# One decoder layer on one core: an input norm without GpSimd, high parts on ScalarE, and three issue points moved

## The chip, the cores and the metric

The kernel runs on one core of a Trainium2 chip. The metric is the device time of one execution in microseconds (us); the time of a kernel is the median of its runs. All rows come from the hardware profiler's record of one execution. PE is TensorE's matmuls, PEld its weight loads, DVE is VectorE, ACT ScalarE, POOL GpSimd, and SPq the queue of SyncE, which issues the transfers.

## The reference

One layer of a decoder, with 1024 tokens and width 1024. What matters here:

```python
h = rmsnorm(x, norm_mix)                       # x * rsqrt(mean(x*x) + eps) * g
fq, fk, fv, ff, su, hq, hf, hi, hg, gl = split(h @ w_in)
y_fox = fox_attention(rmsnorm(fq), rmsnorm(fk), fv, log_sigmoid(ff + b))  # 8 heads x 64, causal
y_s5  = s5_mixer(su, ...)                      # 32 groups, diagonal complex state space, gelu, glu
y_hg  = hgrn2_mixer(hq, hf, hi, hg, ...)       # 4 heads, gated linear recurrence
gates = sigmoid(gl)                            # three of them, 1024 wide each
merged = gates[0]*(y_fox @ wb0) + gates[1]*(y_s5 @ wb1) + gates[2]*(y_hg @ wb2)
x = x + merged @ w_out
x = x + cross_attention(rmsnorm(x), rmsnorm(mem), ...)
x = x + swiglu(rmsnorm(x), w_gate_up, w_down)
```

## The kernel before

Everything is float32 in effect: an operand is split into a high part (a copy rounded to the format that TensorE takes fast, `fp32r`) and a low part (the operand less its high part), and a product of two is three matmuls, high by high, high by low, low by high (`projs`, line 383). The high part is usually a copy on ScalarE and the low part a subtraction on VectorE (`split`, line 264). Tensors lie with channels on the 128 partitions and the 1024 tokens along the free axis; a matmul works on 512 tokens at most. All tiles come from one arena of 50 slots of 128 x 1024 floats (`u`), and all PSUM tiles from 8 banks (`psm`).

The work is written as generators. A main generator (first the state space, then attention, then the recurrence) yields after each stage, with a weight; `drive` (line 334) then calls `pump`, which takes that weight times a constant, in us of matmul work as the program counts it, from a queue of fillers: projections of the normed input, which need nothing of the main line. In this way TensorE has work while VectorE and ScalarE carry a chain. `later(us, fn)` puts off a piece until so much more matmul work has been issued. `ahead(n, fn)` issues a piece under a place n instructions earlier than where it stands. From these places a planner makes the order of instructions on each engine; each engine then works strictly in that order.

The places that the change touches, in order of time:

- `load_x` (line 475) loads the 8 blocks of x one after the other and splits them with the norm's gain. It also forms the sum of squares: for even blocks ScalarE squares and VectorE adds into `acc`, for odd ones GpSimd multiplies and adds into `accg` (named `sq` in the profile). In `run` (line 1342 on) the first two projections, `su0` and `su1`, run over all 8 blocks; behind them `acc` and `accg` are merged and `row_scale` makes the norm's factor `Rb` with a matmul by ones (tile `rs`). All later matmuls stand behind that one.
- `s5_main` (line 1231): for 8 groups of the state space, `s5_prep` (lag 0, GpSimd), `s5_out` (lag 3), `s5_prep2` (lag 1) and `s5_body` (lag 2) are issued in this order in each round o = 0 to 10, and after each the weight `S5_W[lag]` times 4.5 us of fillers. `s5_body` ends with the carried states `kcs` on VectorE, which `s5_out`'s matmuls (tile `s5y`) read one round later. In rounds 8 to 10 there is no `s5_prep`.
- `fox_main` (line 742): 16 units of attention (4 pairs of heads, 2 halves of the queries, 2 heads), each over 4 or 8 blocks of 128 keys. A step is a matmul for the scores (`st`), an exponential on ScalarE (`pf`), its high part on GpSimd and its low part on VectorE (both in `pt`), an addition into the row sums on GpSimd (`facc`), and, two steps later (`PV_LAG`), the matmul with the values (`pv`). The largest score of each row for the next unit is found beside this by `fox_pre` (line 683): matmuls `mx`, maxima on VectorE, then `chain`, four small operations which fill `mc`, and `rows`, which transposes `mc` with TensorE (tile `mt`). After a unit `fox_out` splits the row sums (`ah`), and `sums` adds them over the partitions with a matmul (`sm`).
- `run`, lines 1403 to 1407: gate 1 (branch of the state space) and then gate 2 (branch of the recurrence). Before gate 2, `load_parts` (line 1681) loads the four heads' outputs (`ldy`) and splits them into `yh` and `yl`. In gate 1 GpSimd adds the product into the merged output `mg` through a strided view.

Of the kernel before, what the change touches and what calls it, by code (L numbers as in the profile page):

```python
# [10 lines left out]
F32 = mybir.dt.float32  # L11
# [8 lines left out]
P = 128  # L20
# [32 lines left out]
S5_US = 4.5  # L53
S5_W = (1.0, 0.6, 1.0, 1.2)
FOX_AT = 8
# [17 lines left out]
FOXL_T = 8.0  # L73
MIX_US = 8.5
EPS = 1e-6
NEG = -1e30
# [117 lines left out]
class Trunk:  # L194
# [280 lines left out]
    def load_x(self):  # L475
# [3 lines left out]
        self.xl = [self.u(f"xl{k}", F32R) for k in range(KB)]  # L479
        acc, accg = self.u("acc"), self.u("sq")  # L480
        _, ap, shape = self.wlist[0]
        raw, hi, lo = self.u("wr", F32, shape), self.u("wh", F32R, shape), self.u("wl", F32R, shape)
        self.wraw[0], self.wrdy[0] = raw, (hi, lo)

        def square(k, xk):
            if k % 2 == 0:
                self.sq_add(xk, acc, k, eng=nc.vector)
                return
            sq = accg if k == 1 else self.u("sq")
            self.mul(sq, xk, xk, nc.gpsimd)  # L490
            if k > 1:
                self.add(accg, accg, sq, nc.gpsimd)

        last = None
        for k in range(KB):
            xk = self.u("xk")
            cuts = [slice(0, NT)] if k else [slice(0, 512), slice(512, NT)]
            if k == 0:
                nc.sync.dma_start(out=raw[:, 0:2], in_=ap[:, 0:2])
            for c in cuts:  # L500
                nc.sync.dma_start(out=xk[:, c], in_=self.io["xT"][k][:, c])
            if k == 0:
                nc.sync.dma_start(out=raw[:, 2:], in_=ap[:, 2:])
                self.w_load(1)
                self.split(raw[:, 0:2], hi[:, 0:2], lo[:, 0:2])
            for c in cuts:
                self.split_gain(xk[:, c], self.par("norm_mix", k), self.xh[k][:, c], self.xl[k][:, c])
            if k == 0:
                self.split(raw[:, 2:], hi[:, 2:], lo[:, 2:])
                del self.wraw[0]  # L510
                self.w_prep(1)
            else:
                square(k - 1, last)
            last = xk
        self.w_load(2)
        square(KB - 1, last)
        return acc, accg

# [164 lines left out]
    def fox_pre(self, un):  # L683
# [6 lines left out]
        def build():  # L690
# [4 lines left out]
            st["pm"] = self.sp.tile([P, 4, 2], F32, tag="pmx", name="pmx")  # L695
            st["mn"] = self.sp.tile([P, 4], F32, tag="mn", name="mn")

        def piece(i, c):
# [17 lines left out]
        def chain():  # L716
            mn = st["mn"]
            if half == 1:
                self.nc.vector.tensor_reduce(out=mn, in_=st["pm"], axis=AX.X, op=ALU.max, negate=True)
            mc = self.sp.tile([P, 4, 16], F32, tag="mc", name="mc")  # L720
            mh = self.sp.tile([P, 4], F32R, tag="mh", name="mh")
            self.nc.gpsimd.tensor_copy(out=mc, in_=self.ohc[:, hd].unsqueeze(1).to_broadcast([P, 4, 16]))
            self.nc.vector.tensor_copy(out=mh, in_=mn)
            self.nc.vector.tensor_copy(out=mc[:, :, 8], in_=mh.bitcast(F32))
            self.sub(mc[:, :, 9], mn, mh.bitcast(F32))
            st["mc"] = mc

# [7 lines left out]
        for i in range(4):  # L735
            for c in range(1 if half == 0 else 2):
                out.append(piece(i, c))
        return out + [chain, rows]

    hi_pool = (0, 1, 2, 3)  # L740

    def fox_main(self):
# [11 lines left out]
        for ui, un in enumerate(units):  # L754
# [17 lines left out]
            for j in range(nj):  # L772
# [11 lines left out]
                pt = self.u("pt", F32R).rearrange("p (a b) -> p a b", a=2)  # L784
                if j % 4 in self.hi_pool:
                    self.ts(pt[:, 0, q0:512], pr, 1.0, 0.0, ALU.mult, ALU.add, self.nc.gpsimd)
                else:
                    self.act(pt[:, 0, q0:512], pr, AF.Copy)
                self.sub(pt[:, 1, q0:512], pr, pt.bitcast(F32)[:, 0, q0:512])
# [28 lines left out]
    def fox_out(self, un, o, acc):  # L818
# [26 lines left out]
        if h == 1:  # L845
            self.later(2.0, sums)
        if half == 1 and h == 1:
# [482 lines left out]
    def run(self, stop=None):  # L1330
# [10 lines left out]
        self.plan_rest()  # L1341
        xs = self.load_x()
        self.setup2()
        g = self.projs([(f"su{i}", self.su_evac(i)) for i in range(2)], self.rx)
        for k, _ in enumerate(g):
            if k == 3:
                acc, accg = xs
                self.stt(acc, accg, 1.0 / 1024.0, acc, ALU.mult, ALU.add)
                self.Rb = self.row_scale(acc)
                self.Rt = self.cp.tile([P, 8], F32, name="Rt")  # L1350
                self.later(8.0, lambda: self.col_scale(self.Rb, self.Rt, 8))
        xs = acc = accg = None
        self.filler("su", self.su_projs())
# [48 lines left out]
        zt = None  # L1402
        self.filler("gate1", self.gates(1, ys))
        self.finish()
        ys = None
        self.filler("gate2", self.gates(2, self.load_parts([self.hy_d[h] for h in range(4)])))
        self.finish()
# [248 lines left out]

    def gates(self, b, y):
        for ob in range(8):
            yield from self.gate(b, ob, y)

    def glu(self, zt, y):
# [18 lines left out]

    def load_parts(self, srcs):
        out = []
        for s in srcs:
            t = self.u("ldy")
            self.nc.sync.dma_start(out=t, in_=s)
            h, l = self.u("yh", F32R), self.u("yl", F32R)
            self.split(t, h, l)
            out.append((h, l))
        return out

# [650 lines left out]
```

## Time and profile before

| what | value |
|---|---|
| median of 3 timed runs | 2130.84 us (2130.14 to 2133.14) |
| the profiled execution | 2138.17 us |
| its span, first to last instruction | 2136.1 us |
| mean granted clock of TensorE | 0.992 |
| TensorE busy | 2079.2 us, 97% |
| VectorE busy | 1521.9 us, 71% |
| ScalarE busy | 814.8 us, 38% |
| GpSimd busy | 608.2 us, 28% |

Busy times are sums over the whole span; what an engine waits for is read from the stretch where it waits. A line of a helper such as `mul` or `act` is shared by many operations, so tiles tell them apart. The granted clock is given as a share of full speed (2.4 GHz; 0.50 is 1.2 GHz).

### The profile page before, as it was taken

To read this page: it belongs to the slowest core of one execution; us is meant where nothing else is said; L and a number is where in the kernel's file an instruction comes from. 1 tells how busy PE (TensorE), PEld (TensorE's weight loads), DVE (VectorE), ACT (ScalarE), POOL (GpSimd) and SP (SyncE) were. 2 spreads that over 40 slices of the span, in tenths; PEclk is the share of its full clock that TensorE was granted. 3 is DMA by queue.
4 is the path that set the end of the run, shared out by engine and by line. 5 is a ranking of instruction groups with operands and counts; after the bars stand their busy time and mean duration, and the time that the engine had idled before them with its cause. 6 is when DMAs were issued, how large, how long until landed. Compare 5 with 4: busy or idle time off the path is not lost.

```text
span 2136.1 us, 26862 instructions
## 1 busy us (share of the span) xinstructions
PE 2079.2 (97%) x10044; PEld 1706.7 (80%) x10044; DVE 1521.9 (71%) x2229; ACT 814.8 (38%) x1268; POOL 608.2 (28%) x551
## 2 busy tenths in 40 slices
PE   7998999999999999999999999999999999999999
PEld 5887777776788878888778888878788888888887
DVE  8887898888854566545675567656897778775772
ACT  4113345545531123215434445444533333344441
POOL 4281204454543223221722100011032324221320
PEclk9999999999999999999999999999999999999999
DMA  4332221110213233235554523334232322248582
GB/s 163 137 104 74 51 75 32 40 50 30 70 46 124 73 109 123 74 99 196 194 192 154 201 92 106 119 117 135 74 120 98 124 99 99 103 150 282 189 281 99
DMA packets 121042, 250.94 MB, mean 117 GB/s; under 512 B 15816, under 2 KB 53704, under 8 KB 120912
## 3 DMA queue, kind: packets, MB, share of 16 engines
q1 hardware_dynamic: 120912, 249.23, 34.2%
q8 instruction: 79, 1.29, 0.3%
q14 instruction: 51, 0.42, 0.1%
HBM read 184.83 MB, written 63.18 MB: 116 GB/s over the span
## 4 chain that ended last, share of the span: by engine, by line
PE 59%; DVE 4%; DMA 1%; ACT 1%; issue 0%; SPq 0%; DVEq 0%; ACTq 0%
PE fp L228 27%; PE pj L228 26%; PE hs L228 2%; PE xo L228 1%; PE xs L228 1%; PE rs L228 1%; PE ho L228 0%; DVE t L246 0%; DVE tl L246 0%; DVE gate L246 0%; DMA gate<-gz_d 0%; DVE yl L246 0%; DMA wr<-xv 0%; DMA ldy<-hy_d 0%; PE xt L233 0%
## 5 line engine op out<-in xcount | busy, mean ns | idle before, releaser
L228 PE MATMUL pj<-xl,wh 128*128 128x512 f32 x784 | 315.5, 406 | 4.7 <-DVE xl L258 4.6
L228 PE MATMUL pj<-xh,wh 128*128 128x512 f32 x784 | 313.3, 405 | 6.7 <-ACT xh L243 5.8
L228 PE MATMUL pj<-xh,wl 128*128 128x512 f32 x784 | 311.7, 401 | 0.0
L246 DVE TENSOR_TENSOR wl<-wr,wh 128x1024 fp32r<-128x1024 f32 (+2 forms) x138 | 170.4, 1236 | 58.5 <-ACT wh L243 56.2
L228 PE MATMUL fp<-th,wc 128*128 128x512 f32 x640 | 206.9, 389 | 0.0
L228 PE MATMUL fp<-hh,wc 128*128 128x512 f32 x644 | 191.4, 389 | 0.0
L228 PEld LDWEIGHTS pj<-xh,wh 128*128 128x128 f32 x784 | 149.2, 190 | 40.0 <-ACT xh L243 6.1
L228 PEld LDWEIGHTS pj<-xl,wh 128*128 128x128 f32 x784 | 148.5, 190 | 37.4 <-DVE xl L258 7.1
L228 PEld LDWEIGHTS pj<-xh,wl 128*128 128x128 f32 x784 | 149.1, 190 | 30.8 <-issue 1.9
L228 PE MATMUL fp<-fx,wc 128*128 128x512 f32 x720 | 172.9, 389 | 0.0
L243 ACT ACTIVATE wh<-wr 128x1024 fp32r<-128x1024 f32 (+2 forms) x138 | 131.8, 957 | 76.8 <-DMA wr<-w_in 50.3
L228 PEld LDWEIGHTS fp<-fx,wc 128*128 128x128 f32 x720 | 135.2, 188 | 28.0
L228 PEld LDWEIGHTS fp<-hh,wc 128*128 128x128 f32 x644 | 120.9, 188 | 25.0
L228 PEld LDWEIGHTS fp<-th,wc 128*128 128x128 f32 x640 | 120.2, 188 | 24.9
L246 DVE TENSOR_TENSOR wc<-wr,wc 128x512 fp32r<-128x512 f32 (+1 forms) x116 | 108.5, 954 | 31.4 <-ACT wc L243 31.4
L246 POOL TENSOR_TENSOR dm<-dm 128x256 f32<-128x256 f32 (+1 forms) x96 | 79.5, 828 | 179.9 <-DMA dm<-w_dn 163.0
L246 POOL TENSOR_TENSOR acc<-acc,sq 128x512 f32<-128x512 f32 (+1 forms) x18 | 30.7, 1706 | 340.5 <-ACT sq L243 340.4
L228 PE MATMUL fp<-tl,wc 128*128 128x512 f32 x320 | 124.6, 389 | 0.7 <-DVE tl L246 0.7
L246 DVE TENSOR_TENSOR pt<-pf,pt 128x512 fp32r<-128x512 f32 (+1 forms) x96 | 94.4, 985 | 40.2 <-POOL pt L262 39.9
L246 POOL TENSOR_TENSOR fc<-fc,fs 128x512 f32<-128x512 f32 x40 | 58.0, 1449 | 216.2 <-ACT fs L243 216.2
L228 PE MATMUL fp<-hl,wc 128*128 128x512 f32 x280 | 108.9, 389 | 0.0
L262 POOL TENSOR_SCALAR pt<-pf 128x512 fp32r<-128x512 f32 (+1 forms) x96 | 67.7, 706 | 139.0 <-ACT pf L243 127.8
(427 smaller groups left out, 4862.3 us busy)
## 6 DMA issues: line engine op xcount, KB each, us to landing
wr<-w_in SPq DMA_DIRECT2D x48, 512.0 KB, 4.8
wr<-w_gu SPq DMA_DIRECT2D x44, 512.0 KB, 4.1
hr<-hb_d SPq DMA_DIRECT2D x35, 512.0 KB, 5.4
hb_d<-fc SPq DMA_DIRECT2D x44, 256.0 KB, 2.1
gz_d<-gz SPq DMA_DIRECT2D x20, 512.0 KB, 2.9
dm<-w_dn SPq DMA_DIRECT2D x20, 512.0 KB, 5.6
ws_d<-dm SPq DMA_DIRECT2D x20, 512.0 KB, 3.3
gate<-gz_d SPq DMA_DIRECT2D x20, 512.0 KB, 6.4
```

Of the source, the lines that this page charges most:

```text
L228: self.nc.tensor.matmul(out, lhsT, rhs, start=start, stop=stop)
L243: self.nc.scalar.activation(out=out, in_=in_, func=f, **kw)
L246: return (eng or self.nc.vector).tensor_tensor(out=out, in0=a, in1=b, op=op)
L262: (eng or self.nc.vector).tensor_scalar(out=out, in0=a, scalar1=s1, scalar2=s2, op0=op0, **kw)
```

## The change

Five things. The squares of x go to ScalarE and their adds to VectorE for all blocks, behind the last split, and the merge is gone. The weights after the state space's stages change, from 1.0, 0.6, 1.0, 1.2 to 1.6, 0.6, 1.0, 0.6. In attention the chain behind the row maxima is issued 40 places ahead and GpSimd's copy into `mc` at the unit's start, the sums are put off by 6.0 instead of 2.0 us, and the high part of each exponential is a copy on ScalarE. `load_parts` becomes a generator that gate 1 advances by one step (a load, or a split) after each of its 8 blocks.

```diff
-S5_W = (1.0, 0.6, 1.0, 1.2)
+S5_W = (1.6, 0.6, 1.0, 0.6)
...
+SUM_AT = 6.0
+AH_MAX = 40
...
-        acc, accg = self.u("acc"), self.u("sq")
+        acc = self.u("acc")
...
-        def square(k, xk):
-            if k % 2 == 0:
-                self.sq_add(xk, acc, k, eng=nc.vector)
-                return
-            sq = accg if k == 1 else self.u("sq")
-            self.mul(sq, xk, xk, nc.gpsimd)
-            if k > 1:
-                self.add(accg, accg, sq, nc.gpsimd)
...
-            else:
-                square(k - 1, last)
-            last = xk
         self.w_load(2)
-        square(KB - 1, last)
-        return acc, accg
+        for k, xk in enumerate(xs):
+            self.sq_add(xk, acc, k, eng=nc.vector)
+        return acc
...
             st["mn"] = self.sp.tile([P, 4], F32, tag="mn", name="mn")
+            mc = st["mc"] = self.sp.tile([P, 4, 16], F32, tag="mc", name="mc")
+            self.nc.gpsimd.tensor_copy(out=mc, in_=self.ohc[:, hd].unsqueeze(1).to_broadcast([P, 4, 16]))
...
-            mc = self.sp.tile([P, 4, 16], F32, tag="mc", name="mc")
+            mc = st["mc"]
             mh = self.sp.tile([P, 4], F32R, tag="mh", name="mh")
-            self.nc.gpsimd.tensor_copy(out=mc, in_=self.ohc[:, hd].unsqueeze(1).to_broadcast([P, 4, 16]))
...
-        return out + [chain, rows]
+        return out + [lambda: self.ahead(AH_MAX, chain), rows]
...
-                if j % 4 in self.hi_pool:
-                    self.ts(pt[:, 0, q0:512], pr, 1.0, 0.0, ALU.mult, ALU.add, self.nc.gpsimd)
-                else:
-                    self.act(pt[:, 0, q0:512], pr, AF.Copy)
+                self.act(pt[:, 0, q0:512], pr, AF.Copy)
...
-            self.later(2.0, sums)
+            self.later(SUM_AT, sums)
...
-                acc, accg = xs
-                self.stt(acc, accg, 1.0 / 1024.0, acc, ALU.mult, ALU.add)
                 self.Rb = self.row_scale(acc)
...
-        self.filler("gate1", self.gates(1, ys))
+        yh = []
+        self.filler("gate1", self.gates(1, ys, self.load_parts([self.hy_d[h] for h in range(4)], yh)))
         self.finish()
         ys = None
-        self.filler("gate2", self.gates(2, self.load_parts([self.hy_d[h] for h in range(4)])))
+        self.filler("gate2", self.gates(2, yh))
...
-    def gates(self, b, y):
+    def gates(self, b, y, side=None):
         for ob in range(8):
             yield from self.gate(b, ob, y)
+            if side is not None:
+                next(side, None)
...
-    def load_parts(self, srcs):
-        out = []
+    def load_parts(self, srcs, out):
         for s in srcs:
             t = self.u("ldy")
             self.nc.sync.dma_start(out=t, in_=s)
+            yield
             h, l = self.u("yh", F32R), self.u("yl", F32R)
             self.split(t, h, l)
             out.append((h, l))
-        return out
+            yield
```

## Rows read from the trace of the kernel before

**Rows 1.** The page: the span, the busy times of the engines, and in 40 equal slices the granted clock of TensorE in tenths.

```profile
span 2136.1 us, 26862 instructions
PE 2079.2 (97%) x10044; PEld 1706.7 (80%) x10044; DVE 1521.9 (71%) x2229; ACT 814.8 (38%) x1268; POOL 608.2 (28%) x551
PEclk9999999999999999999999999999999999999999
```

**Rows 2.** The list of waits of TensorE over the whole span: who waited for whom, us in total, how often, the longest.

```profile
PE s5y L228 <- DVE kcs L246: 10.1, 6, 3.3
PE sm L228 <- DVE ah L246: 8.0, 5, 2.3
PE mt L233 <- DVE mc L246: 7.9, 9, 1.7
...
PE pj L228 <- DVE xl L258: 4.6, 2, 3.1
PE pj L228 <- DVE yl L246: 4.1, 2, 3.9
```

**Rows 3.** The table by stretches, for four stretches of lower clock: length, busy time of PE, PEld, DVE, ACT and POOL (instructions), the granted clock, the share of the DMA engines, GB/s.

```profile
168.65:172.06 3.41, 3.26 (x15) 3.26 (x16) 0.69 (x2) 0.00 (x0) 0.00 (x0) 0.50 0.40 159
206.20:213.02 6.82, 6.09 (x21) 5.47 (x22) 5.14 (x14) 2.02 (x4) 0.00 (x0) 0.50 0.06 13
513.40:516.81 3.41, 3.41 (x10) 2.67 (x9) 1.82 (x2) 1.23 (x3) 2.28 (x3) 0.50 0.00 0
1069.77:1076.60 6.83, 5.54 (x13) 4.38 (x14) 4.28 (x3) 0.00 (x0) 6.47 (x6) 0.50 0.01 2
```

**Rows 4.** The timeline of the first 40 us, some of its lines: start, length in us, engine, line, operation, output and inputs, shapes, how many were merged into the row, and in brackets the idle time before.

```profile
11.32 4.72 POOL L246 TENSOR_TENSOR sq<-xk 128x1024 f32<-128x1024 f32 x2
...
11.81 1.04 ACT L243 ACTIVATE acc<-xk 128x1024 f32<-128x1024 f32 x1
11.94 8.55 DVE L258 SCALAR_TENSOR_TENSOR xl<-xk,parT,xh 128x1024 fp32r<-128x1024 f32 x3 [0.75 <-ACT xh L243]
...
12.62 1.91 PE L228 MATMUL pj<-xh,wh 128*128 128x512 f32 x4
12.76 2.17 ACT L243 ACTIVATE xh<-xk,parT 128x1024 fp32r<-128x1024 f32 x2
...
23.24 6.20 DVE L258 SCALAR_TENSOR_TENSOR xl<-xk,parT,xh 128x1024 fp32r<-128x1024 f32 x2
...
35.10 1.21 DVE L246 TENSOR_TENSOR acc<-acc,sq 128x1024 f32<-128x1024 f32 x1
...
36.00 1.08 PE L228 MATMUL pj<-xh,wh 128*128 128x512 f32 x4
36.43 1.23 DVE L258 SCALAR_TENSOR_TENSOR acc<-sq,acc 128x1024 f32<-128x1024 f32 x1
...
36.91 0.61 PE L228 MATMUL pj<-xl,wh 128*128 128x512 f32 x2
...
38.73 1.88 PE L228 MATMUL rs<-acc,cst 128*128 128x512 f32 x4
```

**Rows 5.** The view of one tile, `xk`, in the first 40 us: its loads (shortest, median and longest issue in ns, first and last start in us), and the time from issue to landing.

```profile
L501 SPq DMA_DIRECT2D xk<-xT x9: 328/442/944, 1.6 to 8.8; - x9
...
DMA to landing us min/median/max: 3.3/8.7/10.0
```

**Rows 6.** The timeline of TensorE, around three matmuls of the state space's outputs that waited.

```profile
168.80 0.80 PE L228 MATMUL s5y<-kcs,s5x 128*128 128x128 f32 x2 [2.62 <-DVE kcs L246]
...
206.93 0.80 PE L228 MATMUL s5y<-kcs,s5x 128*128 128x128 f32 x2 [3.34 <-DVE kcs L246]
...
249.93 0.49 PE L228 MATMUL s5y<-kcs,s5x 128*128 128x128 f32 x2 [1.33 <-DVE kcs L246]
```

**Rows 7.** The table by stretches, for the state space (with the parameters behind it) and for attention; columns as in rows 3.

```profile
120.00:320.00 200.00, 188.51 (x979) 154.48 (x978) 174.65 (x269) 66.33 (x94) 56.48 (x41) 0.97 0.26 73
320.00:600.00 280.00, 260.65 (x1254) 204.36 (x1253) 233.88 (x376) 150.40 (x251) 137.59 (x169) 0.99 0.13 45
```

**Rows 8.** Groups of instructions from 335 to 650 us, shapes kept apart, one view each for VectorE, ScalarE and GpSimd: busy us, mean ns of one, and idle time before them.

```profile
L246 DVE TENSOR_TENSOR pt<-pf,pt 128x512 fp32r<-128x512 f32 x47 | 60.9, 1300 | 30.8 <-POOL pt L262 30.7
...
L246 DVE TENSOR_TENSOR ah<-facc,ah 128x512 fp32r<-128x512 f32 x16 | 11.8, 740 | 0.3
...
L243 ACT ACTIVATE ah<-facc 128x512 fp32r<-128x512 f32 x16 | 10.0, 626 | 0.7 <-DVE pt L246 0.5
...
L262 POOL TENSOR_SCALAR pt<-pf 128x512 fp32r<-128x512 f32 x47 | 34.9, 744 | 62.7 <-ACT pf L243 57.0 <-DVE pt L246 2.3 <-DVE ah L246 2.2
L246 POOL TENSOR_TENSOR facc<-facc,pf 128x512 f32<-128x512 f32 x24 | 34.7, 1446 | 4.6 <-ACT pf L243 4.6
```

**Rows 9.** The timeline around one wait for the row maxima.

```profile
330.93 0.68 DVE L709 TENSOR_REDUCE mn<-mx 128x1 f32<-128x512 f32 x1
...
331.53 0.82 DVE L246 TENSOR_TENSOR pt<-pf,pt 128x256 fp32r<-128x256 f32 x1
...
333.07 0.28 PE L233 MATMUL mt<-cst,mc 128*16 128x128 f32 x1 [1.20 <-DVE mc L246]
```

**Rows 10.** Groups of instructions from 1020 to 1080 us, where gate 1 ends and gate 2 begins; columns as in rows 8.

```profile
L246 POOL TENSOR_TENSOR mg<-mg,gate 128x512 f32<-128x512 f32 x16 | 37.6, 2390 | 19.0 <-DVE gate L246 19.0
...
L246 DVE TENSOR_TENSOR yl<-ldy,yh 128x1024 fp32r<-128x1024 f32 x4 | 9.1, 2275 | 3.4 <-ACT yh L243 3.4
```

More of the change, by code (lines that the diff above doesn't have):

```diff
@@ L483, in load_x @@
         self.wraw[0], self.wrdy[0] = raw, (hi, lo)
-        def square(k, xk):
-            if k % 2 == 0:
-                self.sq_add(xk, acc, k, eng=nc.vector)
-                return
-            sq = accg if k == 1 else self.u("sq")
-            self.mul(sq, xk, xk, nc.gpsimd)
-            if k > 1:
-                self.add(accg, accg, sq, nc.gpsimd)
-        last = None
+        xs = []
         for k in range(KB):
             xk = self.u("xk")
+            xs.append(xk)
             cuts = [slice(0, NT)] if k else [slice(0, 512), slice(512, NT)]
@@ L725, in chain @@
             self.sub(mc[:, :, 9], mn, mh.bitcast(F32))
-            st["mc"] = mc
         def rows():
@@ L737, in fox_pre @@
                 out.append(piece(i, c))
-        return out + [chain, rows]
-    hi_pool = (0, 1, 2, 3)
+        return out + [lambda: self.ahead(AH_MAX, chain), rows]
     def fox_main(self):
@@ L1341, in run @@
         self.plan_rest()
-        xs = self.load_x()
+        acc = self.load_x()
         self.setup2()
@@ L1351, in run @@
                 self.later(8.0, lambda: self.col_scale(self.Rb, self.Rt, 8))
-        xs = acc = accg = None
+        acc = None
         self.filler("su", self.su_projs())
```

## The prediction

> **What bounds the kernel now.** I read the profile's page first. TensorE is busy for 97% of the span and has no stretch of its own that stands empty; every other engine has room on average [rows 1]. So the time is TensorE's work, which this change leaves as it is, plus the time in which TensorE stands idle or runs at half clock. The span less its busy time is 2136.1 - 2079.2 = 56.9 us [rows 1]. The list of who waited for whom, for TensorE alone, says where most of that is: the state space outputs wait 10.1 us for `kcs`, the attention sums 8.0 us for `ah`, the transposes of the row maxima 7.9 us for `mc`, the first projections 4.6 us for the low parts of x, and the third gate 4.1 us for `yl` [rows 2]. These five are 34.7 us, and each of the change's moves is aimed at one of them. The table by stretches adds a second price: the granted clock was 0.50 of full speed in four stretches, and each begins within 2 us of one of those gaps [rows 3]. In such a stretch TensorE loses half of its busy time: 3.26/2 = 1.6 us, 6.09/2 = 3.0, 3.41/2 = 1.7 and 5.54/2 = 2.8, in all 9.1 us [rows 3]. So 43.8 us is what the moves can be worth at most by these rows, and I now go through how much of it each one gets.
>
> The profiled execution took 2138.17 us (span 2136.1), 7.3 us over the median of the three timed runs, 2130.84. The terms below come from the profile; I subtract them from the median, since they are small shares that should be alike in both.
>
> **Input norm.** It removes four GpSimd squares and three GpSimd adds and one merge on VectorE, adds four squares on ScalarE and four adds on VectorE (all 8 and 7 now lie there), and puts them behind the last split of x. While GpSimd ran its squares, three `xl` took 8.55 us and two took 6.20, 2.85 and 3.10 each; the same operation of the same size without GpSimd beside it, the merge, took 1.23 [rows 4]. The next limit is the arrival of x: its last load is issued at 8.8 us and loads take at most 10.0 us to land, so 18.8 [rows 5]; a split needs 1.09 on ScalarE (2.17 for two) and 1.23 on VectorE [rows 4], so `xl` of block 7 is there by 21.1. TensorE is far behind that: its second step starts at 12.62 and 84 matmuls remain. Start to start four matmuls take 36.91 - 36.00 = 0.91, 0.228 each [rows 4]; 84 x 0.228 = 19.2, and the first four there take 1.91 where later ones show 1.08, 0.8 more, which gives 32.6. Now the norm's matmul starts at 38.73 [rows 4]. So 6.1 us, if the sum of squares is ready at 32.6: ScalarE 18.8 + 1.1 + 8 x 1.04 = 28.2, the last add 1.21, so 29.4. Were a weight's split (1.1 there, 1.2 here) put in front it would be 31.7, still covered by 0.9; what lies beyond that costs its own length, because this matmul stands in front of all others. I take **6.0**, bounds 3.5 (one more split and a slow add) to 6.5.
>
> **State space outputs later.** The weights 1.0, 0.6, 1.0, 1.2 become 1.6, 0.6, 1.0, 0.6, the sum is the same. After `s5_prep` there is 0.6 x 4.5 = 2.7 us more of projection work before `s5_out`. Of the six gaps three lie where a prep stands ahead: 2.62, 3.34 and 1.33 [rows 6]; they fall to 0, 0.6 and 0. The other three, 10.1 - 7.3 = 2.8 us, belong to the last groups, which have no prep ahead; they stay. From `s5_out` to `s5_body` 2.7 us less work stands, so VectorE reaches the body's chain with more in its queue; VectorE is busy 174.65 of 200 us there [rows 7], so I let the gaps grow by 1.0 in all. That is 2.62 + 2.7 + 1.33 - 1.0 = 5.6. Both clock drops here follow the two long gaps (4.6 us); I take 3.6 of it, as the gap of 0.6 that is left may still bring one. **9.2**, bounds 2 (VectorE keeps its pace, the gaps come back at the next wait) to 10.3.
>
> **Row maxima ahead.** The four small VectorE operations behind the last maximum come 40 places earlier, and GpSimd's copy into `mc` moves to the start of the unit. In a wait of 1.20 us the last maximum began at 330.93 and a subtraction of 0.82 stood between it and the chain [rows 9]: without that, 0.4 is left. What cannot move is the maximum itself. I take 60% of 7.9, **4.7**, bounds 2 (the maximum ends last) to 7.
>
> **Sums later.** 6.0 instead of 2.0 us of matmul work after the unit. The five waits are 8.0 us, the longest 2.3 [rows 2], all under the 4.0 that are added. What they wait for (add on GpSimd, split on ScalarE and VectorE) does not move back. **7.9**, bounds 5 to 8.4. The clock drop at 513.40 follows one of them; I take **1.5** of its 1.7, bounds 0 to 1.7.
>
> **High parts on ScalarE.** 92 of the 96 lie in the stretch shown. GpSimd takes 0.744 us for a full block. For ScalarE's price I take the same copy of `facc`, 0.626 [rows 8]; by columns for the narrower ones 47 x 0.626 + 15 x (0.47 + 0.31 + 0.16) = 44 us. ScalarE is busy 150.40 of 280 us [rows 7]; so 0.54 becomes 0.69. The path from exponential to low part was 0.744 + 1.300 = 2.04 [rows 8]. VectorE's 1.300 is long because GpSimd's addition into `facc`, 1.446, runs beside it (the same subtraction on `ah` takes 0.740) [rows 8]. That addition now starts at once, while the copy lasts 0.63, so it still covers most of the subtraction: about 1.45 + 0.69 = 2.1 at the latest, 0.63 + 0.74 = 1.4 at best. I take no relief for VectorE. The page SBUF — State Buffer of the Trainium skill, section Who interferes with whom, states that the operation of GpSimd or VectorE that starts second waits until the first has ended. By it this part gives VectorE nothing; by a reading in which a free GpSimd means a free VectorE it would give 47 x 0.6 = 28 us of VectorE's time. The startup rows agree with the page in direction (2.85 against 1.23), not in size. The cost is on ScalarE: exponentials queue behind copies and behind the five copies of a new unit. Two steps of lag cover this mostly. **-2.0**, bounds -10 (two full copies, 1.25, uncovered in each of the 8 units that start with such a burst) to +3 (the path falls to 1.4 and waits for `ah` and `mc` shrink with it).
>
> **Recurrence output beside the second gate.** The four loads, copies and subtractions come one half at a time behind blocks of gate 1. Waits of 4.1 us and 2.8 us of clock are at stake. The four subtractions took 2.275 us on average against 1.23 alone, since GpSimd works through 16 strided adds of 2.390 us in those 60 us [rows 10]. The last subtraction is still issued at the gate's end, so up to 1.5 us may remain. **5.5**, bounds 2 to 6.9. The loads go through SP's queue ahead of weights for the next block; the list of TensorE's waits has none for a transfer there, so I charge nothing, and a weight that comes late would show as a wait for `wl` in gate 1, at most the length of one load.
>
> **Sum.** 6.0 + 9.2 + 4.7 + 7.9 + 1.5 - 2.0 + 5.5 = 32.8. The order on each engine is made anew by a planner from changed places, and I leave 3.0 for small waits that are not there now. 2130.84 - 29.8 = **2101.0**. All terms at their good ends: 43.8, so 2087; all at their bad ends, 4.5: 2126.
>
> **Rivals.** First, **VectorE sets the pace**: it is busy 233.88 of 280 us in attention and 174.65 of 200 before it [rows 7], so a wait taken from one place comes back at the next. Then input norm (6.0) and gate (5.5) stand, the sums give 4, the maxima 2, the outputs 3 without clock, less 2.0 and 3.0: 15.5, **2115**. For it: VectorE is the last to release all five waits. Against: it has 46 us of room in attention. The second, on the other side, is **ScalarE as gate of attention**: if each copy delays the next exponential and the lag does not hide it, its 44 us come onto the path; less the 34.8 of the other parts and with the 3.0 left for small waits, the kernel would take 2130.84 + 44 - 34.8 + 3.0 = 2143. It turns slower once over 31.8/44 = 0.7 of the copies' time shows. Against it: 0.69 busy, and TensorE waited only 7.9 + 8.0 us in the whole stretch, none of it long for an exponential. The third is that **the order does not move**: the 40 places change nothing because the maximum ends last, and the later outputs are late again; without 4.7 and with 3 of 9.2 it is 2112, and I count it with the first.
>
> **Chances.** The forecast, 2094 to 2109: 0.53. Better than that, to 2087: 0.08. VectorE's pace or an order that doesn't move, 2109 to 2125: 0.27. Within 0.2% (4.3 us, about what a measurement of this kernel can tell from no change): 0.05. Slower, ScalarE's queue: 0.07. So faster 0.88. The range 2089 to 2121 leaves out some 2 in 10.
>
> **What would show it.** Right: `xl` at 1.2 to 1.3 us and the norm's matmul near 33 us; no wait over 1 us for `kcs` before the last three groups, and none for `ah`; `mc` under 4 us in all; ScalarE near 0.7 busy in attention with few waits of TensorE for `pt`; the third gate starting with a gap under 1.5 us; full clock at all four places. Wrong: a norm matmul waiting for `acc`; `kcs` waits as long as now; new TensorE waits for `pt`, `q12a` or weights of 10 us or more; the subtraction on `pt` at 0.7 us, which would give VectorE the room that I left out.

## The result, and the profile after

| | before | after |
|---|---|---|
| median, four runs each | 2131.99 us (2130.14 to 2133.97) | 2145.7 us (2142.15 to 2148.56) |
| profiled execution, and its span | 2138.17, 2136.1 | 2142.15, 2140.3 |
| TensorE busy | 2079.2 | 2078.3 |
| VectorE, ScalarE, GpSimd busy | 1521.9, 814.8, 608.2 | 1500.2, 865.9, 537.6 |

The ratio of the times is 1.0063, with a 95% interval of 1.0044 to 1.0082: slower by 0.6%, some 13 us, where I forecast 1.4% faster. The two profiled executions are only 4.2 us apart, since that of before lay 6 us above its median and that of after 3.5 below, so I use them for where time goes and the medians for how much. TensorE's busy time is that of before, so what was lost is time in which it was idle or ran at half clock, which counts as busy too. The list of waits of TensorE in the kernel after (who waited for whom, us in total, how often, the longest) answers to [rows 2]:

```profile
PE s5y L230 <- DVE kcs L248: 13.7, 5, 4.2
PE pj L230 <- DVE wl L248: 6.4, 4, 4.0
PE mt L235 <- DVE mc L248: 6.2, 5, 3.2
...
PE pv L230 <- DVE pt L248: 3.4, 4, 2.1
PE mx L230 <- DVE pmx L705: 3.2, 1, 3.2
...
PE hst L230 <- ACT hbT L245: 3.0, 1, 3.0
...
PE rs L230 <- ACT sq L245: 2.5, 1, 2.5
...
PE sm L230 <- DVE ah L248: 1.6, 1, 1.6
```

The waits for `xl` and `yl` are gone and that for `ah` has fallen from 8.0 to 1.6, as forecast. That for `kcs` has grown from 10.1 to 13.7, and `wl`, `pt`, `pmx`, `hbT` and `sq` are new or longer.

**Input norm and gates went as forecast in this trace.** From the timeline of the first 40 us after the change, beside [rows 4]:

```profile
12.52 8.97 DVE L260 SCALAR_TENSOR_TENSOR xl<-xk,parT,xh 128x1024 fp32r<-128x1024 f32 x7 [0.81 <-ACT xh L245]
...
30.16 1.22 DVE L248 TENSOR_TENSOR acc<-acc,sq 128x1024 f32<-128x1024 f32 x1
31.29 1.22 DVE L248 TENSOR_TENSOR wl<-wr,wh 128x1024 fp32r<-128x1024 f32 x1
...
33.17 1.88 PE L230 MATMUL rs<-acc,cst 128*128 128x512 f32 x4
```

Seven `xl` take 8.97/7 = 1.28 us each, and the norm's matmul starts at 33.17 instead of 38.73: 5.6 us. In the table by stretches (length; busy time of PE, PEld, DVE, ACT, POOL with instructions; granted clock; share of the DMA engines; GB/s) the stretch of the gates has no gap and no half clock, where [rows 3] had 0.50:

```profile
1040.00:1080.00 40.00, 40.00 (x178) 33.15 (x177) 35.28 (x26) 11.40 (x15) 37.24 (x21) 1.00 0.49 170
```

By these rows some 12 us came in (5.6 at the norm, and the 4.1 and 2.8 of the gates). With a median that is 13 us slower, some 25 must have gone out elsewhere.

### The profile page after: what moved, and what is told of

Its sections match the earlier page's. It is cut to its first block, busy times and chain, and to the rows that moved or that the text cites. A ratio compares the mean times of both kernels' runs of the same rounds, so it can differ in the third digit from the quotient of the medians.

```text
span 2140.3 us, 26931 instructions
## 1 busy us (share of the span) xinstructions
PE 2078.3 (97%) x10044; PEld 1708.4 (80%) x10044; DVE 1500.2 (70%) x2232; ACT 865.9 (40%) x1369; POOL 537.6 (25%) x448
## 4 chain that ended last, share of the span: by engine, by line
PE 71%; DVE 6%; ACT 3%; issue 1%; DMA 0%; DVEq 0%; ACTq 0%; SPq 0%
PE pj L230 35%; PE fp L230 27%; PE hs L230 2%; PE rs L230 1%; PE st L230 1%; PE xo L230 1%; PE xs L230 1%; PE pv L230 1%; PE ho L230 1%; PE mx L230 0%; DVE t L248 0%; DVE pt L248 0%; DVE tl L248 0%; DVE wl L248 0%; ACT sq L245 0%
## 5 line engine op out<-in xcount | busy, mean ns | idle before, releaser
L230 PEld LDWEIGHTS pj<-xl,wh 128*128 128x128 f32 x784 | 149.2, 190 | 30.9 <-issue 3.4
L248 POOL TENSOR_TENSOR dm<-dm 128x256 f32<-128x256 f32 (+1 forms) x96 | 86.0, 896 | 156.9 <-DMA dm<-w_dn 108.5
L248 POOL TENSOR_TENSOR facc<-facc,pf 128x256 f32<-128x256 f32 (+1 forms) x64 | 70.0, 1094 | 123.8 <-ACT pf L245 118.0
L248 DVE TENSOR_TENSOR pt<-pf,pt 128x512 fp32r<-128x512 f32 (+1 forms) x96 | 73.4, 767 | 39.3 <-ACT pt L245 38.9
```

The source lines that it names most:

```text
L230: self.nc.tensor.matmul(out, lhsT, rhs, start=start, stop=stop)
L248: return (eng or self.nc.vector).tensor_tensor(out=out, in0=a, in1=b, op=op)
```

## The experiments

All ratios are to the kernel before on the same chip, with 95% intervals. I turn them into us by 2132, so that runs of different chips can be compared; a difference of two such numbers is uncertain by 4 to 5 us. The theories that the expectations name are those under test at that point.

**Undoing parts.** First the old weights, in the changed kernel: `-S5_W = (1.6, 0.6, 1.0, 0.6)`, `+S5_W = (1.0, 0.6, 1.0, 1.2)`:

> The changed kernel (2145.7 us) with the old weights 1.0, 0.6, 1.0, 1.2 after the state space's stages; all else as changed. Theory 1 (the new weights put GpSimd's s5_prep beside VectorE's scans and starve the last groups: 8.6 us in the stretch from 120 to 320 us and what spills into the attention's start): 2133 to 2137, the waits of s5y for kcs near 10 us again, the four scans at 1.4 us. Theory 2 (the copies on ScalarE are the loss): 2143 to 2146. Theory 3 (any new order of the planner scatters small gaps): no side, within 3 us of 2145.

2124.92 us, ratio 0.9968 (0.9956 to 0.9980). So the weights alone cost 0.0095 x 2132 = 20.3 us. Then the new weights again, but the high parts back on GpSimd:

```diff
-                self.act(pt[:, 0, q0:512], pr, AF.Copy)
+                self.ts(pt[:, 0, q0:512], pr, 1.0, 0.0, ALU.mult, ALU.add, self.nc.gpsimd)
```

> The changed kernel with the high parts of the exponentials back on GpSimd; all else as changed. Theory 1 (state space weights): 2143 to 2147, nothing gained, since GpSimd's load was no bound. Theory 2 (the copies on ScalarE delay exponentials and the splits of new units; about 10 us in attention): 2134 to 2137, and the waits for pt and pmx (6.6 us together) gone.

2148.61 us, 1.0070 (1.0057 to 1.0082): no gain, so theory 2 falls. Both edits together:

> The changed kernel with both taken back: the old weights and the high parts on GpSimd; the input norm, the maxima ahead, the later sums and the recurrence output beside gate 1 stay. By my forecast's terms for those four (6.0 + 4.7 + 9.4 + 5.5 less 3.0 of 2132.0): 2109. By theories 1 and 2 together, each with its loss from the traces (2145.7 - 8.6 - 10): 2127. Theory 3 (planner's chance): 2130 or more.

2131.91 us, 0.9983 (0.9972 to 0.9994). The four parts that are left bring hardly anything, though nothing of theories 1 and 2 is in them. And with the maxima and the sums taken back too, which leaves input norm and gates:

> The kernel before (2132.0) with only the input norm without GpSimd and the recurrence output beside gate 1. By the traces (5.6 us at the norm's matmul, 6.9 at the gates) 2119.5; by my forecast's terms (6.0 + 5.5) 2120.5. If what is saved at the start comes back as gaps in the state space, as the changed kernel's stretch from 120 to 320 us could also be read: 2125 or more.

2124.43 us, 0.9956 (0.9943 to 0.9969): 9.4 us of the forecast 11.5, the same within the uncertainty. Maxima and sums together are therefore a loss, not a gain. How the 9.4 divide is not shown: in this run's trace the third gate does not start without a gap, as it did in the change. The wait for `yl` is gone, but two others stand in its place, and the clock from 1040 to 1080 us is 0.96 (0.91 before, 1.00 in the change):

```profile
1063.45 0.50 PE L230 MATMUL pj<-yh,wl 128*128 128x512 f32 x1 [2.49 <-DVE wl L248]
...
1070.71 0.50 PE L230 MATMUL pj<-yh,wh 128*128 128x512 f32 x1 [1.98 <-ACT wh L245]
```

**Where the weights lose.** First, new weights in some rounds only. In the first run `S5_X` holds the old weights; the second is its mirror image, with the old weights up to round 7:

```diff
-                    yield S5_W[lag] * (...)
+                    yield (S5_W if o < 8 else S5_X)[lag] * (...)
```

> The changed kernel (2145.7 us) with the new weights 1.6, 0.6, 1.0, 0.6 in rounds 0 to 7 and the old 1.0, 0.6, 1.0, 1.2 in rounds 8 to 10, where no s5_prep stands. The old weights in all rounds gave 2124.9. Theory 1a (the loss of 20 us is in the last rounds: without s5_prep its raised weight is never issued, so some 10.8 us of matmul work are missing there and VectorE's queue decides): 2122 to 2128, and only the waits of groups 5 to 7 get short. Theory 1b (the loss is GpSimd's s5_prep beside VectorE's scans in the middle rounds): 2140 or more, the scans still at 3 to 5 us.

2148.8 us, 1.0069 (1.0051 to 1.0087).

> The counterpart: the changed kernel with the old weights in rounds 0 to 7 and the new ones in rounds 8 to 10. Theory 1a (the last rounds): 2138 to 2145, with the waits of 2 to 4 us for kcs, wl and mc between the last bodies as in the changed kernel. Theory 1b (the middle rounds): 2124 to 2128.

2136.04 us, 1.0013 (1.0002 to 1.0024). Theory 1a falls as worded: old weights in the last rounds cure nothing, though new ones there alone cost 9.6 us too (one wait of TensorE of 7.3 us, for `qmm` at the start of attention). Theory 1b, GpSimd beside VectorE's scans in the middle rounds, is still open here. A third placing, `S5_W = (1.0, 0.6, 1.6, 0.6)`:

> The changed kernel with the weights 1.0, 0.6, 1.6, 0.6: what was taken behind s5_out stands behind s5_body, so in front of the next round's outputs in all rounds, with the same sum in each round that has a body. If what the outputs need is only more work between s5_body and the next s5_out, the 10.1 us of kcs waits of the old weights fall to 3 or less: 2114 to 2118. If VectorE has to get through the output's work before the body (theory 1a, its cause): the waits stay near 10 us or grow, 2124 to 2135.

2131.57 us, 1.0000 (0.9988 to 1.0012), some 7 us worse than the old weights; its three longest waits for `kcs` are still 2.6, 2.3 and 1.8 us.

What the changed kernel and the run with new weights up to round 7 have in common became clear from the program's own count of issued matmul work (in its own us), taken when some stages are issued:

```
                        old     new     new, rounds 0-7   old, early factor 2.79
output of group 0     120.2   134.4   134.4             131.9
output of group 5     223.0   236.3   236.3             236.3
output of group 7     257.3   263.7   265.0             265.0
projections used up   266.7   266.7   266.7             266.7
```

The projections for this stage are a fixed list, used up at 266.7 with either weights. With the old ones 43.7 are left when the output of group 5 is issued, with the new ones 30.4. The 13 in between went out in rounds 0 to 2: `s5_out` isn't there yet, so its lowered weight is never counted, while the raised one of `s5_prep` is, in the first two rounds times 1.75. Next, the new weights only in rounds 3 to 7, where all four stages stand (`S5_W if 3 <= o < 8 else S5_X`):

> The changed kernel with the new weights in rounds 3 to 7 alone, where all four stages stand, and the old ones in rounds 0 to 2 and 8 to 10. Theory 1c (the projections are a fixed store that the state space uses up: the new weights spend 0.6 x 4.5 x 1.75 x 2 + 2.7 = 12.15 us more of it in rounds 0 to 2, where TensorE had no gap, and that much is missing behind the last bodies): the loss of 20 us is gone; 2116 if the outputs in the middle get their forecast 9.2 us, 2122 to 2126 if that move is worth nothing. Theory 1b (GpSimd beside the scans in the middle rounds): 2138 or more.

2128.26 us, 0.9981 (0.9968 to 0.9993): 17 of the 20 us are gone, and theory 1b falls with them. The move that the forecast had in mind is worth nothing (2.8 us slower than the old weights, within the uncertainty); the outputs wait as before:

```profile
PE s5y L231 <- DVE kcs L249: 10.8, 6, 3.3
```

With the new weights and other factors at the ends (`S5_BEG` 1.04, `S5_END` 2.59):

> The changed kernel with its new weights in all rounds, but the factor of the first two rounds 1.04 instead of 1.75 and that of the last two 2.59 instead of 1.5, so that the first three and the last three rounds issue as much matmul work as with the old weights. Theory 1c: as the run with the new weights in rounds 3 to 7 alone, 2116 to 2126, 20 to 30 us under the changed kernel with the same four weights. Theories that blame the order of the stages itself (1b, or the end rounds' short way from output to body): 2138 or more.

2136.97 us, 1.0018 (1.0007 to 1.0028): 9.6 us better than the change, but no better than before, and a miss: 2116 to 2126 was expected. Its count is that of the run before it at the output of group 5 (223.0), and 261.2 instead of 257.3 at that of group 7. So nearly equal amounts bring back only half of the loss; what the rest is, no run shows. And the other way round, the weights of before and only the phase shifted (on the kernel of the first experiment, `S5_BEG` 1.75 to 2.79):

> The changed kernel with the old weights (2124.9 us) and the factor of the first two rounds 2.79 instead of 1.75, so that 2.6 x 4.5 x 1.04 = 12.2 us more matmul work is issued in these rounds and, the store being the same, 12.2 less behind the last bodies. Theory 1c (early spending): 2137 to 2146, with waits of 2 to 6 us behind the last three bodies near 310 to 335 us, as in the changed kernel. If the order of outputs, prep and body in a round is the cause: 2123 to 2128.

2150.41 us, 1.0083 (1.0062 to 1.0103). With the old weights the loss is back, at 24.5 us, so the new order of the weights within a round is not needed for it; the phase is enough. The gaps are the same seven, in the same order, though not of the same size. Timeline of TensorE, rows with a long idle time before them (start, length, ..., in brackets the idle time and what ended it), the change:

```profile
177.05 0.80 PE L230 MATMUL s5y<-kcs,s5x 128*128 128x128 f32 x2 [4.21 <-DVE kcs L248]
...
236.96 0.79 PE L230 MATMUL s5y<-kcs,s5x 128*128 128x128 f32 x2 [3.11 <-DVE kcs L248]
...
270.45 1.55 PE L230 MATMUL rs<-sq,cst 128*128 128x512 f32 x2 [2.45 <-ACT sq L245]
...
309.32 0.49 PE L230 MATMUL s5y<-kcs,s5x 128*128 128x128 f32 x2 [1.99 <-DVE kcs L248]
...
315.59 0.80 PE L230 MATMUL pj<-xh,wl 128*128 128x512 f32 x1 [3.96 <-DVE wl L248]
...
326.17 0.80 PE L230 MATMUL s5y<-kcs,s5x 128*128 128x128 f32 x2 [3.80 <-DVE kcs L248]
...
333.64 1.02 PE L235 MATMUL mt<-cst,mc 128*16 128x128 f32 x4 [3.25 <-DVE mc L248]
```

and the old weights with the raised early factor:

```profile
177.44 0.80 PE L230 MATMUL s5y<-kcs,s5x 128*128 128x128 f32 x2 [3.42 <-DVE kcs L248]
...
238.02 0.80 PE L230 MATMUL s5y<-kcs,s5x 128*128 128x128 f32 x2 [3.13 <-DVE kcs L248]
...
271.26 1.40 PE L230 MATMUL rs<-sq,cst 128*128 128x512 f32 x2 [2.45 <-ACT sq L245]
...
312.07 0.49 PE L230 MATMUL s5y<-kcs,s5x 128*128 128x128 f32 x2 [3.94 <-DVE kcs L248]
...
317.02 0.79 PE L230 MATMUL pj<-xh,wl 128*128 128x512 f32 x1 [1.51 <-DVE wl L248]
...
328.73 0.49 PE L230 MATMUL s5y<-kcs,s5x 128*128 128x128 f32 x2 [3.55 <-DVE kcs L248]
...
335.14 1.01 PE L235 MATMUL mt<-cst,mc 128*16 128x128 f32 x4 [2.27 <-DVE mc L248]
```

The table by stretches shows where the time goes; first the change, then its counterpart with the old weights (the first experiment):

```profile
0.00:120.00 120.00, 112.68 (x493) 91.11 (x494) 90.23 (x230) 36.33 (x39) 32.38 (x57) 1.00 0.43 154
120.00:280.00 160.00, 149.61 (x761) 122.66 (x760) 119.81 (x179) 51.51 (x75) 43.88 (x33) 0.96 0.22 62
280.00:340.00 60.00, 47.00 (x233) 39.01 (x232) 55.69 (x102) 21.57 (x31) 3.34 (x4) 0.89 0.25 77
```

```profile
0.00:120.00 120.00, 112.81 (x504) 91.20 (x505) 97.84 (x235) 36.46 (x40) 32.65 (x56) 1.00 0.43 148
120.00:280.00 160.00, 150.49 (x792) 122.73 (x791) 136.81 (x210) 53.97 (x79) 49.97 (x36) 0.98 0.25 71
280.00:340.00 60.00, 57.09 (x287) 45.70 (x286) 54.12 (x104) 33.80 (x55) 5.43 (x8) 1.00 0.23 71
```

Busy time by clock is TensorE's work done. From 280 to 340 us that is 47.00 x 0.89 = 41.8 against 57.1: 15.3 us lost. From 120 to 280 it is 143.6 against 147.5: 3.9. Together 19.2 of the 20.3. In the change the state space's first output starts at 149.2 us instead of 132.5 and its last at 328.7 instead of 306.1. In those last 60 us VectorE is busy 55.69 of 60, but so it is in the counterpart (54.12); the difference lies in front of them, where up to 280 us it has been busy 24.6 us less in the change and had 40 us of room from 120 on. I read this so: the same work of bodies, outputs and attention's set-up comes later and has 13 us less of projections beside it, and VectorE's pace then shows as gaps of TensorE.

**The other direction.** If 12 us more in the first rounds cost 20, do 6 us less there gain? On the best kernel so far (of the group below), `S5_BEG` 1.25 with `S5_END` 1.88, and `S5_BEG` 1.25 with a factor of 1.07 in rounds 3 to 8:

> The best so far (2116.9: input norm, recurrence output beside gate 1, high parts on ScalarE, maxima ahead, old weights) with the first factor 1.25 instead of 1.75 and the last 1.88 instead of 1.5, which moves 5.8 us of matmul work from the first two rounds to the last two. Theory 1c, if the last bodies still lack work there: the waits behind them (0.9, 1.2 and 0.7 us for kcs) go, 2113 to 2116. If the early rounds need their work after all, TensorE shows gaps from 80 to 160 us and the time is 2117 to 2122.

2145.08 us, 1.0061 (1.0044 to 1.0078).

> The same base (2116.9) with the first factor 1.25 and a factor of 1.07 in rounds 3 to 8, which gives each of them 1.2 us more matmul work: 6 us moved from the first two rounds to the rounds in which the waits for kcs stand (2.6, 3.3, 1.3, 0.9 and 1.2 us). If matmul work in these rounds is what is short: each of these waits falls by up to 1.2 us, 2111 to 2115. If VectorE's order decides and not the amount: the waits stay, 2115 to 2120.

2138.09 us, 1.0028 (1.0016 to 1.0039). Both miss what I expected by 18 us and more: they are 29 and 22 us slower than their base. Other things wait here; in the second, with a wait of 5.9 us for `kcs` at 250.51, the clock from 240 to 280 us is 0.79. From the timeline of the first of the two, TensorE and then ScalarE:

```profile
102.91 0.95 PE L235 MATMUL s5g<-cst,s5x 128*128 128x128 f32 x4 [1.96 <-POOL s5x L248]
...
106.27 0.55 PE L230 MATMUL s5k<-s5x 128*16 128x112 f32 x2 [2.25 <-POOL s5x L248]
...
298.00 2.07 PE L230 MATMUL rs<-sq,cst 128*128 128x512 f32 x2 [9.79 <-ACT sq L245]
```

```profile
297.31 0.63 ACT L245 ACTIVATE sq<-qs 128x512 f32<-128x512 f32 x1 [9.01 <-DVE qs L248]
```

At the start GpSimd's preparation now comes too late for its matmuls. At the end a projection of attention (`qs`, with a norm of its own: VectorE, ScalarE, then the matmul `rs`) has fallen into the last bodies, and its row of `qs` stands in VectorE's order behind a whole body; another such `rs` waits 7.4 us at 268.40. So the amount of matmul work that is left is not all; which projection meets which stage counts too.

**Maxima, sums and high parts, in all combinations.** With old weights, input norm and gates in all of them. Base: 0.9956. The expectations stand in this order: maxima, then sums, with GpSimd's copies; then ScalarE's copies alone, with the maxima, with the sums.

> The kernel before with input norm and recurrence output beside gate 1 (2124.4) and the row maxima's chain ahead; high parts on GpSimd. By the forecast's term 4.7: 2119.7. If the gain needs a VectorE that ScalarE's copies have relieved: 2123 to 2127.

> The kernel before with input norm and recurrence output beside gate 1 (2124.4) and the sums 6.0 us later; high parts on GpSimd, so that all 8.0 us of waits for ah are there to be taken. By the forecast's term 9.4 with clock: 2115. If the new places bring the waits for pt, pmx and hbT (about 8 us) here too: 2123 to 2130, while the waits for ah fall to about 1 us.

> The kernel before with the input norm, the recurrence output beside gate 1 (these two gave 2124.4) and the high parts on ScalarE; maxima, sums and weights as before. If the copies on ScalarE are a gain by themselves (they were one of 7 us among the earlier maxima and later sums, 2131.9 to 2124.9): 2117 to 2120. If they only pay for what the maxima and sums cost: 2123 to 2126. By my forecast's term of -2.0: 2126.

> The kernel before with input norm, recurrence output beside gate 1, high parts on ScalarE (these gave 2122.1) and the row maxima's chain 40 places ahead. By the forecast's term 4.7: 2117.5. If the waits for mc (6.9 us without it) fall but come back as waits for pmx and pt, 3.3 us each with it, and clock: 2122 to 2127.

> The kernel before with input norm, recurrence output beside gate 1, high parts on ScalarE (2122.1) and the sums 6.0 us later. ScalarE's copies had already cut the waits for ah from 8.0 to 2.6 us (the low parts on VectorE take 1032 ns instead of 1321), so by that at most 2.6 to 4.0 are left: 2118 to 2121. By the forecast's term 9.4 with clock: 2113. If the wait for hbT at about 737 us (3.0 us, in each kernel with later sums and maxima so far) belongs to the sums, it shows here and not with the maxima alone, and the sum is 2120 to 2124.

| high parts on | neither | maxima ahead | sums at 6.0 | both |
|---|---|---|---|---|
| GpSimd | 2124.43, 0.9956 | 2125.66, 0.9968 (0.9955 to 0.9980) | 2131.61, 0.9991 (0.9979 to 1.0002) | 2131.91, 0.9983 |
| ScalarE | 2122.13, 0.9947 (0.9928 to 0.9966) | 2116.92, 0.9924 (0.9909 to 0.9938) | 2124.15, 0.9952 (0.9938 to 0.9967) | 2124.92, 0.9968 |

Along each line of the table, in us: the high parts on ScalarE gain 1.9, 9.4, 8.3 and 3.2, on average 5.7 (uncertain by about 2). The sums cost 7.5, 3.2, 1.1 and 9.4, on average 5.3, no less uncertain. The maxima give -2.6, 4.9, 1.7 and -3.4: nothing on average. The 4.9, with the copies and without the sums, is just within its uncertainty, and the wait for `mc` fell by 1.0 only (6.9 to 5.9). That pair, without sums and weights, is the best kernel here: 0.76% faster than before.

Why the sums cost: the waits of TensorE with the sums alone on the base, where `ah` was 8.0 and the other three were not in the list:

```profile
PE pv L230 <- DVE pt L248: 4.3, 6, 1.4
...
PE mx L230 <- DVE pmx L703: 3.2, 1, 3.2
PE hst L230 <- ACT hbT L245: 3.0, 1, 3.0
...
PE sm L230 <- DVE ah L248: 0.9, 1, 0.9
```

The 7.1 us that `ah` gives up come back as 10.5, which is 3.4 of the 7.5 us. Some of the rest is clock: from 340 to 660 us TensorE was busy for 302.54 us at 1.00 on the base and is for 301.29 at 0.98 here. The waits of 3.2 for `pmx` and 3.0 for `hbT` stand in all kernels here with sums at 6.0 but one (new weights from round 8), and in none with sums at 2.0. One more, sums at 4.0 on the best kernel:

> The same base (2116.9) with the sums 4.0 instead of 2.0 us later. If the cost of the later sums grows with the delay (8 us at 6.0 beside the earlier maxima): 2119 to 2122. If it comes with a particular new order of the planner's (the waits of 2.1 us for pt, 3.2 for pmx and 3.0 for hbT, the same in all five kernels with 6.0): either none of them or all of them, 2115 to 2117 or 2123 to 2126.

2123.4 us, 0.9954 (0.9940 to 0.9968). By time this does not decide: 6.4 us of cost at 4.0 beside 9.4 at 6.0 leaves room for an even growth (4.7). By the waits it does: `pmx` doesn't wait here, `hbT` waits its 3.0 as ever, so they do not come as one whole. The later place makes the planner deal the order anew, as far as the recurrence at 745 us, more than 100 us behind the last sum. Why it deals just so is not settled.

Why the copies gain: VectorE's subtraction for the low parts of a full block, from 335 to 650 us, with GpSimd's copies (base) and then with ScalarE's (groups by form: count, busy us and mean ns, idle time before it and what ended it):

```profile
L248 DVE TENSOR_TENSOR pt<-pf,pt 128x512 fp32r<-128x512 f32 x46 | 60.6, 1321 | 30.2 <-POOL pt L264 30.0
```

```profile
L248 DVE TENSOR_TENSOR pt<-pf,pt 128x512 fp32r<-128x512 f32 x46 | 47.2, 1032 | 30.3 <-ACT pt L245 29.8
```

VectorE gets 13.4 us back from these alone, and the wait for `ah` falls from 8.0 to 2.6 (that for its half on ScalarE grows from 0.4 to 1.4) with the sums where they were. The two means hide how it comes about. The timeline shows one block with GpSimd's copy, and then the same block with ScalarE's and a later one that GpSimd leaves alone:

```profile
350.10 0.62 POOL L264 TENSOR_SCALAR pt<-pf 128x512 fp32r<-128x512 f32 x1 [2.32 <-ACT pf L245]
350.68 1.29 POOL L248 TENSOR_TENSOR facc<-facc,pf 128x512 f32<-128x512 f32 x1
350.75 1.76 DVE L248 TENSOR_TENSOR pt<-pf,pt 128x512 fp32r<-128x512 f32 x1 [1.72 <-POOL pt L264]
```

```profile
350.48 0.63 ACT L245 ACTIVATE pt<-pf 128x512 fp32r<-128x512 f32 x1
350.60 1.30 POOL L248 TENSOR_TENSOR facc<-facc,pf 128x512 f32<-128x512 f32 x1 [1.93 <-ACT pf L245]
...
351.15 1.29 DVE L248 TENSOR_TENSOR pt<-pf,pt 128x512 fp32r<-128x512 f32 x1 [1.22 <-ACT pt L245]
...
371.09 0.69 DVE L248 TENSOR_TENSOR pt<-pf,pt 128x512 fp32r<-128x512 f32 x1 [0.89 <-ACT pt L245]
```

Both of the long subtractions end 0.54 us after GpSimd's addition; the free one takes 0.69. So it is throughout: of the 46, 33 begin while GpSimd is in an operation with GpSimd's copies, 28 with ScalarE's, and all but one in each end 0.53 to 0.56 us after that operation; the others take 0.67 to 0.70. With ScalarE's copies the addition starts when the exponential ends, while the copy still runs, and the subtraction behind the copy finds less of it left, 0.76 us on average instead of 1.07. That this relief of VectorE is what makes the kernel faster is read from the traces; no run parts it from the rest of the move.

## Why the prediction was wrong

- **Input norm (6.0) and recurrence output (5.5)**: right as a sum, 9.4 us by the ratio, and 33.17 for the matmul forecast at 32.6. The last add ended at 31.38, not 29.4, since seven adds in a row on VectorE took 1.3 us each, and a weight's split stood behind it (31.29); both were covered. That the gates give 5.5 by themselves is not shown: without the other parts waits of 2.5 and 2.0 us stood there.
- **State space outputs (9.2)**: the step that failed, and the one that turned the sign: "The weights 1.0, 0.6, 1.0, 1.2 become 1.6, 0.6, 1.0, 0.6, the sum is the same." It is the same only where all four stages stand. In rounds 0 to 2 the new ones issue 0.6 x 4.5 x 1.75 x 2 + 2.7 = 12.15 us more, which is missing at the end. The loop that skips stages and the factors of the first rounds stood in the code. Without this shift the term would not have been 9.2 but about 0: in rounds 3 to 7 alone the waits for `kcs` are 10.8 us, as before. I took it that 2.7 us more of work in front of an output shortens its gap by as much; the gaps of 2.62, 3.34 and 1.33 were 3.31, 3.34 and 1.33 with it. Against the sum: 9.4 for the first 11.5, -20.3 for this 9.2, and -2.6 for the 12.1 of the three parts in attention, together the 13 us of loss.
- **Row maxima ahead (4.7)**: nothing by itself (`mc` 7.3 us against 7.8), and 4.9 with the copies, which `mc` (6.9 to 5.9) does not explain. The first rival fits: VectorE is behind, and an earlier place in its order doesn't make it faster.
- **Sums later (7.9 + 1.5)**: the wait for `ah` fell as forecast, but the 3.0 for "small waits that are not there now" was the mis-sized term: three new waits of this part alone are 10.5 us.
- **High parts on ScalarE (-2.0)**: wrong in sign, +5.7 on average. "I take no relief for VectorE" failed: the subtraction went from 1321 to 1032 ns. The page SBUF — State Buffer of the Trainium skill, section Who interferes with whom, states that a VectorE operation with two inputs in SBUF and a GpSimd operation that reads SBUF exclude each other: the second waits for the first to end. The trace agrees, operation by operation, as the 0.53 to 0.56 us above show. What was wrong is what I drew from it, that this part gives VectorE nothing: a subtraction waits only for what is left of the addition, and that is what the part shortened. The 740 that I took for one alone [rows 8] is a mean that holds some such waits too; alone it takes 0.69 us. Nor do the startup rows disagree with the page in size, as I wrote: each of the five `xl` beside GpSimd ended 1.08 to 1.09 us after the GpSimd operation in which it began, where one alone takes 1.28. The second rival, ScalarE as gate, had the right side of 2132, and with 2143 nearly the time, by luck: with GpSimd's copies the changed kernel is not faster (1.0070).
- **The whole**: the first rival's mechanism, VectorE's pace, comes nearest to what the traces show, but I priced it at some 14 us of lost gains and gave it no way to lose. Of the ways of being slower only one was on the list, ScalarE's queue, and it was not what happened.

Open: how the 20.3 us of the shift divide between work that is missing at the end and meetings such as GpSimd's beside the scans (below); both come with the phase, and no run parts them. The scans' part seems small: with the old weights and the early factor 2.79 the longest four took 3.27 us, not 5.12, and the loss was no smaller.

## What to carry to other kernels

Where filler work comes from a fixed list, a weight moved from one stage to another is a shift of phase between two streams in all rounds in which one of the stages is missing: sum the weights over the whole loop, first and last rounds too, before the sum of one round is called the same. A tuned phase can be narrow on both sides: 12 us one way and 6 the other each cost 20 us or more here. When work is taken from an engine, ask too when the next work on it will start: here VectorE got its time back largely from an addition that began earlier. And test parts one by one, then in combination: of six parts two lost, one forecast as a loss gained, and one brought nothing by itself.

## What the hardware showed unexpectedly

Four scans of VectorE on 128x128, 1.36 us with nothing on GpSimd (the kernel with old weights, at 158.03), took 5.12 in the change, where GpSimd's preparation fell beside them:

```profile
168.02 1.71 POOL L248 TENSOR_TENSOR s5x<-s5x,s5tm 128x512 f32<-128x512 f32 x1
169.81 1.06 POOL L248 TENSOR_TENSOR s5tm<-s5pw,s5cx 128x512 f32<-128x512 f32 x1
170.95 1.28 POOL L248 TENSOR_TENSOR s5x<-s5x,s5tm 128x512 f32<-128x512 f32 x1
172.31 1.05 POOL L248 TENSOR_TENSOR s5tm<-s5rv,s5bx 128x512 f32<-128x512 f32 x1
```

```profile
168.53 5.12 DVE L1179 TENSOR_TENSOR_SCAN s5dd<-s5rv,s5dd 128x128 f32<-128x128 f32 x4
```

Each of the four begins while one of GpSimd's operations runs and ends 0.28 us after it. That is 3.8 us in the chain that ends in `kcs`, and the wait of 4.21 us at 177.05 follows it.
